# Seven block products for eight in a two-layer decoder trunk on one Trainium2 core

## The chip, the cores and the metric

The kernel runs on one core of one Trainium2 chip. The metric is device time in microseconds, from one launch to its end. In the profile PE is the matrix engine, PEld its weight loads (they overlap PE), DVE the vector engine, ACT the scalar engine, POOL the general engine, and SP the engine whose queue issues this kernel's DMAs.

## The reference: what is computed

A trunk of two residual layers over 2048 tokens of width 1024, float32, then a final normalisation. The second layer, which the change rewrites, uses dilated window attention in three groups of (window, dilation) and six heads of 128; each group has q, k and v of its own. Both layers also attend to 256 memory tokens with four heads of 64, multiply everything by a SiLU gate and project back. Cut to that layer:

```python
DIL_GROUPS = ((128, 1), (512, 4), (2048, 16))
def dilated_mixer(h, w_in):
    for g, (window, dil) in enumerate(DIL_GROUPS):
        base = g * 3 * 768
        qkv = (h @ w_in[:, base:base + 2304]).reshape(B, T, 3, 6, 128)
        q = partial_rope(qkv[:, :, 0], pos)      # rotates the first 32 of 128 rows of a head
        k = partial_rope(qkv[:, :, 1], pos)
        o, lse = dilated_group(q, k, qkv[:, :, 2], window, dil)
        ...
    wts = softmax(stack(lses), axis=0)           # over the three groups
    o = einsum('gbth,gbthd->bthd', wts, outs)
    q_mem, gate = split(h @ w_in[:, 6912:], [256])
# for each layer:
    branch = concat([mix, mem_o]) * silu(gate)
    x = x + branch @ w_out[i]
```

The second layer's input projections are a product of 2048 x 1024 by 1024 x 8192: 6912 columns for q, k and v, 256 for the memory queries, 1024 for the gates.

## The kernel before

Precision is kept by splitting each float32 operand into a high and a low fp16 half. `mm3` (L174 to L177) then makes one product of three matmuls: high by high, high by low, low by high.

**First layer** (to 913.7 us). Gated linear attention in blocks of 128 tokens, then a second pass over the 16 blocks: memory queries and memory attention (`a2_q`), gates (`a2_gate`), the branch transposed on PE (`a2_branch`), the output projection (`a2_out`). `a2_h2` normalises the block, transposes it on PE (`split_T`, L162) and writes it, split, into `h2T`, which stays in SBUF for the whole second layer.

**Second layer, units** (913.7 to about 2264 us). A unit is a pair of heads and a group, nine in all, in the order of three head pairs by three groups. For each:

- `load_qk` and `load_v` fetch three weight blocks of 1024 x 256 through the one buffer `stg` and split them (`load_w`: squares for a scale, then high and low).
- `proj_qk` projects q and k for one head: weights stationary, 512 tokens moving, 24 matmuls for each of four token chunks. The first 32 rows are rotated chunk by chunk (DVE L808, POOL L809, DVE L810 and L811), and the halves go to SBUF in the group's order (ACT L813, DVE L814).
- `proj_v` projects v for both heads: tokens stationary (every 1st, 4th or 16th, by the group), 256 weight columns moving, 24 matmuls for each of 16 blocks, evicted by ACT L786 and DVE L787.
- `attend` does one head in blocks of 128 queries against one or two blocks of keys: scores, masked maximum (DVE L843), exponential (ACT L854), split into halves (ACT L168, POOL L169), a DMA transpose through SP (L170), and the product with v. Results go to DRAM (`o_d`, L875).

Program order in a unit is attention of the first head, projection of the second head's q and k, attention of the second head, projections of the next unit. The framework's planner orders each engine's instructions by priority in program order and by a timeline of its own, so projections fill the waits of attention.

**Gates.** `gate_prep` works out the three groups' weights for a head pair. `gate_item` makes one head and chunk of 512 tokens: 24 matmuls, SiLU, then the three groups' results are read back (`og`) with their weights (`fb`), multiplied (POOL L940 and L945, DVE L942), summed (DVE L948, L949), multiplied by the gate (DVE L951) and stored. There are 24 such items. Eight are placed in unit (1, 0), eight in the last unit and eight in the stage after it, where the 16 blocks of memory attention and eight gate items of the memory heads stand too (2264 to 2520 us).

**Output** (2520 us to the end). 16 blocks of 128 tokens by 1024 columns in a rounded float32 type, three matmuls a product, then the residual and the final normalisation. Half of its weights are fetched in the stage before.

All DMAs go through SP's queue, in order.

Of the kernel before, what the change touches and what calls it, by code (L numbers as in the profile page):

```python
# [16 lines left out]
P = 128  # L17
# [17 lines left out]
def trunk(ctx, tc, a, out):  # L35
# [38 lines left out]
    cols = tl(cp, [P, 160], F32, "cols")  # L74
# [99 lines left out]
    def mm3(o, sh, sl, mh, ml, first, last):  # L174
        PE.matmul(o, sh, mh, start=first, stop=False)  # L175
        PE.matmul(o, sh, ml, start=False, stop=False)  # L176
        PE.matmul(o, sl, mh, start=False, stop=last)  # L177
# [58 lines left out]
    def mem_scores(mem, q2, wk, tg, hls):  # L236
# [3 lines left out]
        for j in range(4):  # L240
            PE.transpose(t[:, j * P:(j + 1) * P], q2[:, j].rearrange("p a d -> p (a d)"), id16)
# [4 lines left out]
        for hh in range(2):  # L246
# [9 lines left out]
            p_ = tl(wk, [P, 512], F32, tg[1 + hh])  # L256
# [58 lines left out]
    f_d = [tl(dram, [4, 3, 512], F32, f"fd{h}") for h in range(6)]  # L315
    kv_d = tl(dram, [2, 4, P, 512], F16, "kvd")
    br_d = [tl(dram, [P, 4, KT, P], F32, f"brd{c}") for c in range(4)]


    pa_ctx = ctx.enter_context(ExitStack())  # L320
    wp = pa_ctx.enter_context(pool("wpa", 5))
# [281 lines left out]
    h2T = tl(h2p, [P, 2, KT, T], F16, "h2T")  # L603

    with ExitStack() as c2:
        wo_p = c2.enter_context(pool("wo", 1, "right"))
# [11 lines left out]
        def a2_q(b):  # L618
# [6 lines left out]
            mem_pv(mem0, mem_scores(mem0, qm, k2, ("qmT", "mp", "mpt"), ((stg, "stg"), (sga, "stg"))), om, ps_g)  # L625
# [35 lines left out]
        def a2_out(b, bT, it):  # L661
            cj = tl(sp, [P, 4], F32, "cj")
            V.tensor_scalar(out=cj, in0=iwo, scalar1=it, scalar2=None, op0=ALU.mult)
            xt = tl(k1, [P, D], F32, "x")
# [12 lines left out]
        def a2_h2(b, xt):  # L677
            r = rstd_of(rowss(xt, k2), 1, D)
            xn = tl(k1, [P, D], F32, "sg")
            V.scalar_tensor_tensor(out=xn, in0=xt, scalar=r, in1=nw1, op0=ALU.mult, op1=ALU.mult)  # L680

            def emit(k0, k1_, t):
                tv = t.rearrange("p (k n) -> p k n", n=P)
                hi = h2T[:, 0, k0:k1_, b * P:(b + 1) * P]
                A.activation(out=hi, in_=tv, func=AF.Copy)
                V.tensor_tensor(out=h2T[:, 1, k0:k1_, b * P:(b + 1) * P], in0=tv, in1=hi, op=ALU.subtract)
            split_T(xn, KT, emit)
# [10 lines left out]
        xt = None  # L698
        for b in range(NB):
            bT = a2_branch(b, om, gt[0], gt[1])  # L700
            it = gt[2]
            if b + 1 < NB:
                hT, om = a2_q(b + 1)
                gt = a2_gate(hT)
            xo = a2_out(b, bT, it)
            if b > 0:
                a2_h2(b - 1, xt)
            xt = xo
        a2_h2(NB - 1, xt)
    pa_ctx.close()  # L710

# [457 lines left out]
```

## Time and profile before

| what | value |
|---|---|
| median of 2 runs | 2721.89 us (2721.33 to 2722.46) |
| profiled execution: time | 2715.5 us |
| its span, first to last instruction | 2713.5 us |
| granted TensorE clock, mean | 0.989 |
| PE busy | 2603.2 us (96%), 19166 matmuls |
| DVE, ACT, POOL busy | 1510.0, 1128.4, 496.9 us |
| DMA | 259.23 MB, mean 96 GB/s |

A row of a stretch gives its start and end, its length, then for each engine the busy time and, as x, the instructions; then the granted clock, the mean busy share of the 16 DMA engines and GB/s. A row of a group gives line, engine, operation, output <- inputs, shapes and count; after the bar the busy time in us and the mean ns of one; after the second bar the engine's idle time just before them and what ended it. Matmuls are pipelined, so the mean duration of one is longer than the distance to the next. A row of a timeline gives start and duration in us, the idle time before it in brackets. A row of one line gives the least, median and largest duration in ns and the first and last start. A row of waits gives the total, the times and the longest.

### The profile page before, as it was taken

The page shows a single profiled execution, that of the slowest core. Times are in us where ns is not written, and L with a number is a line of the kernel's source. Part 1 is how long each engine was busy: PE and PEld are TensorE (multiplying, and loading weights), DVE is VectorE, ACT ScalarE, POOL GpSimd, SP SyncE. Part 2 cuts the span into 40 slices and gives each one's busy share as a digit, 9 for nine tenths or more (in the row PEclk, how much of TensorE's full clock was granted, in tenths as well). Part 3 has the DMA queues.
Part 4 walks back from the last instruction along what each step waited for, and adds up shares of the span by engine and source line. Part 5 has one row for each costly group of instructions (what it writes and reads, how often), then busy time and mean ns, then how long its engine had stood idle before and what let it go on. Part 6 is the DMA issues. An engine that isn't in the chain of part 4 may idle for free. (4 is left out here: it accounts for less than half of the span.)

```text
span 2713.5 us, 47912 instructions
## 1 busy us (share of the span) xinstructions
PE 2603.2 (96%) x19166; PEld 1937.0 (71%) x19166; DVE 1510.0 (56%) x3349; ACT 1128.4 (42%) x2621; POOL 496.9 (18%) x421
## 2 busy tenths in 40 slices
PE   7999999999999999999999998999999999788999
PEld 6889998899988845858475474756667574455687
DVE  6445443665555466373746637465555637777433
ACT  6356444543434434252425324243433434535322
POOL 0000000010101023131313314222222313443000
PEclk9999999999999999999999999999999999899999
DMA  5242113333332213130313535122322224776543
GB/s 202 84 143 74 65 57 94 119 90 96 91 96 81 91 47 86 34 90 26 87 53 100 121 86 135 38 68 73 78 62 62 72 65 128 197 172 139 158 148 114
DMA packets 377539, 259.23 MB, mean 96 GB/s; under 512 B 250674, under 2 KB 340452, under 8 KB 377316
## 3 DMA queue, kind: packets, MB, share of 16 engines
q1 hardware_dynamic: 377316, 256.17, 33.7%
q8 instruction: 150, 2.46, 0.4%
q14 instruction: 73, 0.60, 0.1%
HBM read 149.63 MB, written 60.21 MB: 77 GB/s over the span
## 5 line engine op out<-in xcount | busy, mean ns | idle before, releaser
L175 PE MATMUL ps_mm<-w,hT 128*128 128x256 f16 (+1 forms) x1408 | 387.2, 275 | 3.7 <-DVE ws L128 1.8
L176 PE MATMUL ps_mm<-w,hT 128*128 128x256 f16 (+1 forms) x1408 | 385.9, 275 | 0.0
L177 PE MATMUL ps_mm<-w,hT 128*128 128x256 f16 (+1 forms) x1408 | 385.2, 275 | 0.4 <-DVE hT L370 0.4
L175 PE MATMUL ps_mm<-h2T,w 128*128 128x512 f16 x944 | 359.2, 380 | 0.5 <-DVE qm L232 0.4
L177 PE MATMUL ps_mm<-h2T,w 128*128 128x512 f16 x944 | 358.8, 380 | 0.6 <-DVE cols L306 0.6
L176 PE MATMUL ps_mm<-h2T,w 128*128 128x512 f16 x944 | 358.9, 380 | 0.0
L809 POOL TENSOR_TENSOR sh<-sh,rope 32x512 f32<-32x512 f32 x144 | 183.2, 1272 | 629.8 <-DVE sh L808 623.3
L177 PEld LDWEIGHTS <-w 128*128 128x128 f16 x1408 | 139.1, 99 | 148.1 <-issue 3.0
L175 PEld LDWEIGHTS <-w 128*128 128x128 f16 x1408 | 138.5, 98 | 144.5 <-issue 2.4
L176 PEld LDWEIGHTS <-w 128*128 128x128 f16 x1408 | 138.5, 98 | 144.0 <-issue 2.8
L175 PE MATMUL ps_mm<-w,h2T 128*128 128x256 f16 x840 | 229.2, 273 | 0.5 <-DVE sg L301 0.5
L176 PE MATMUL ps_mm<-w,h2T 128*128 128x256 f16 x840 | 229.5, 273 | 0.0
L177 PE MATMUL ps_mm<-w,h2T 128*128 128x256 f16 x840 | 229.4, 273 | 0.0
L854 ACT ACTIVATE pm<-pm,st,cols 128x256 f32<-128x256 f32 (+1 forms) x288 | 156.2, 543 | 135.7 <-DVE st L848 134.6
L169 POOL TENSOR_TENSOR ph<-pm,ph 128x512 f16<-128x512 f32 (+2 forms) x144 | 143.5, 1001 | 291.5 <-issue 158.8
L175 PE MATMUL ps_x<-h2T,w 128*128 128x512 f16 x464 | 177.4, 382 | 0.3 <-DVE v L787 0.3
L176 PE MATMUL ps_x<-h2T,w 128*128 128x512 f16 x464 | 177.2, 382 | 0.0
L177 PE MATMUL ps_x<-h2T,w 128*128 128x512 f16 x464 | 177.1, 382 | 0.0
L169 POOL TENSOR_TENSOR stg<-mp,stg 128x512 f16<-128x512 f32 x16 | 18.5, 1159 | 833.9 <-DMA ogd<-og 457.7
L176 PEld LDWEIGHTS <-h2T 128*128 128x128 f16 x1280 | 149.4, 117 | 10.1 <-issue 2.5
L175 PEld LDWEIGHTS <-h2T 128*128 128x128 f16 x1280 | 149.5, 117 | 7.7
L176 PEld LDWEIGHTS <-hT 128*128 128x128 f16 x1408 | 138.8, 99 | 22.3 <-issue 4.1
(317 smaller groups left out, 6102.4 us busy)
## 6 DMA issues: line engine op xcount, KB each, us to landing
stg<-in_w_in_b SPq DMA_DIRECT2D x64, 512.0 KB
od<-osb SPq DMA_DIRECT2D x72, 256.0 KB
og<-od SPq DMA_DIRECT2D x72, 256.0 KB
fb<-fd SPq DMA_DIRECT2D x24, 768.0 KB
x<-in_x SPq DMA_DIRECT2D x32, 512.0 KB
hTd<-hT SPq DMA_DIRECT2D x16, 512.0 KB
hT<-hTd SPq DMA_DIRECT2D x16, 512.0 KB
x1d<-x SPq DMA_DIRECT2D x16, 512.0 KB
```

The source lines that it names most:

```text
L169: G.tensor_tensor(out=lo, in0=src, in1=hi, op=ALU.subtract)
L175: PE.matmul(o, sh, mh, start=first, stop=False)
L176: PE.matmul(o, sh, ml, start=False, stop=False)
L177: PE.matmul(o, sl, mh, start=False, stop=last)
L809: G.tensor_tensor(out=sw, in0=sw, in1=rs, op=ALU.mult)
L854: A.activation(out=p_, in_=p_, func=AF.Exp, scale=sc, bias=st[:, j:j + 1], accum_out=st[:, 16 + j:17 + j])
```

## The change

The second layer's projections become one level of a seven-product block scheme. Tokens are cut into chunk pairs, the contraction of 1024 into two halves, and 256 weight columns into two halves of 128. A half of the tokens (`hf`) takes chunks `hf` and `hf + 2`.

- `a2_pair` replaces `a2_h2`. It takes blocks m and m + 8 together, so the blocks run in the order 0, 8, 1, 9 and so on; POOL forms the sums, ACT and DVE split seven operands in `stg` and `sga`, and DMA transposes put them in place. Some go by way of DRAM (`h2_d`).
- `load_ws` replaces `load_w256` in the second layer: a weight block becomes seven split operands of 512 x 128, in a pool of nine tiles. POOL forms the sums. q and k of one head make one block, so `load_qk` is called per head.
- `sw_half` does the seven products of a half, each of 48 matmuls of 128 columns (values, memory queries) or 12 of 512 (q, k, gates), in three PSUM banks, with snapshots and sums between them. `mm_bank` turns over four banks, among them `ps_tr`, which the transposes had alone.
- `proj_qk` collects the 32 rows to be rotated from four results into one tile of 128 partitions and rotates them together. q, k and v are written to DRAM (`qk_d`, `vu_d`) and read back by `att_load` in pieces of four blocks. In the third group a piece holds every fourth token, and `blk` reads it with a step of 4.
- The value projection's moving operand has 128 columns, and its stationary rows have steps of 1 or 4.
- All gate items, the memory queries and memory attention stand in a last stage after the units, in the order written out below; `fb` and `og` are a third of their size, with two buffers each. The output weights are fetched in the output stage, and its blocks run in another order.

```diff
+        def a2_pair(m, x1, x2):
+            ha = tl(stg, [P, 4, 2, 512], F16, "stg")
+            hb = tl(sga, [P, 3, 2, 512], F16, "stg")
+            ...
+            def put(o, src):
+                hl = ha[:, o] if o < 4 else hb[:, o - 4]
+                A.activation(out=hl[:, 0, :], in_=src, func=AF.Copy)
+                V.tensor_tensor(out=hl[:, 1, :], in0=src, in1=hl[:, 0, :], op=ALU.subtract)
+                fl = hl.rearrange("p a n -> p (a n)")
+                ...
+                    SY.dma_start_transpose(h2s[0][o].rearrange("p a k t -> p (a k) t")[:, :, ts], fl)
+                else:
+                    t = tl(k1, [P, 8, P], F16, "tq")
+                    SY.dma_start_transpose(t, fl)
+                    ...
+    OPS = (0, 4, 1, 5, 3, 2, 6)
+    def load_ws(srcs, invh, joint=True, cps=None):
+        raw = tl(stg, [P, KT, 256], F32, "stg")
+        ...
+        def put(n_, src):
+            ...
+            A.activation(out=t[:, 0], in_=src, func=AF.Copy, scale=s1)
+            V.scalar_tensor_tensor(out=t[:, 1], in0=src, scalar=s1, in1=t[:, 0], op0=ALU.mult, op1=ALU.subtract)
+        put(0, b11)
+        G.tensor_tensor(out=b11, in0=b12, in1=b11, op=ALU.subtract)
+        put(4, b11)
+        ...
+    def sw_half(ops, hf, wst, g, fin):
+        def pr(t, n, first):
+            w, h = ops[n], h2s[hf][OPS[n]]
+            if wst:
+                for k in range(4):
+                    mm3(t, w[:, 0, k, :], w[:, 1, k, :], h[:, 0, k, :], h[:, 1, k, :], first and k == 0,
+                        k == 3, True)
+                return
+            for m in range(4):
+                for k in range(4):
+                    mm3(t[:, m * P:(m + 1) * P], hcols(h[:, 0, k, :], g, m), hcols(h[:, 1, k, :], g, m),
+                        w[:, 0, k, :], w[:, 1, k, :], first and m == 0 and k == 0, m == 3 and k == 3, True)
+        ...
+        ta = mm_bank()
+        pr(ta, 0, True)
+        p1 = snap(ta, "p1")
+        tb = mm_bank()
+        pr(tb, 1, True)
+        u2 = snap(tb, "u2")
+        G.tensor_tensor(out=u2, in0=u2, in1=p1, op=ALU.add)
+        pr(ta, 2, False)
+        fin(ta, 0, 0, True)
+        pr(tb, 3, False)
+        u3 = snap(tb, "u3")
+        G.tensor_tensor(out=u3, in0=u3, in1=p1, op=ALU.add)
+        tc_ = mm_bank()
+        pr(tc_, 4, True)
+        x22 = addto(tc_, u3)
+        fin(x22, 1, 1, False)
+        pr(tb, 5, False)
+        x21 = addto(tb, p1)
+        fin(x21, 1, 0, False)
+        pr(tc_, 6, False)
+        x12 = addto(tc_, u2)
+        fin(x12, 0, 1, False)
+    def store_cols(d, g, c, hl, rows, r0):
+        if g == 0:
+            SY.dma_start(d[c][rows].rearrange("p a j x -> p a (j x)"), hl[r0])
+        else:
+            for e in range(2):
+                SY.dma_start(d[:, rows, e, c, :].rearrange("j p x -> p j x"),
+                             hl[r0, e, :].rearrange("p (j x) -> p j x", j=4))
+    def gate_item(hp, sg, c, i):
+        acc = None
+        for g in (2, 1, 0):
+            fb = tl(gb, [P, 16, 32], F32, "fb")
+            ...
+            og = tl(gb, [P, 512], F32, "og")
+            ...
+            if acc is not None:
+                V.tensor_tensor(out=fb, in0=fb, in1=acc, op=ALU.add)
+            acc = fb
         sv = sg.rearrange("p (l q) -> p q l", q=16)
         V.tensor_tensor(out=sv, in0=acc, in1=sv, op=ALU.mult)
     for n, u in enumerate(units):
+        w1_ = load_qk(u, 1)
+        attend(u, 0, wqk)
+        proj_qk(u, 1, w1_)
+        ...                      # weights of the next unit
+        attend(u, 1, w1_)
+        if not last:
+            proj_qk(units[n + 1], 0, wqk)
+            proj_v(units[n + 1], wv)
+    qm_half(0)
+    qm_half(1)
+    gate_prep(0)
+    gw = load_gate(7168)
+    mem_chunk(0)
+    gate_half(gw, 0, lambda sg, c, i: gate_item(0, sg, c, i))
+    mem_chunk(2)
+    gate_half(gw, 1, lambda sg, c, i: gate_item(0, sg, c, i))
+    ...                          # the second head pair in the same way
+    gate_half(wg, 0, mem_item)
+    gate_half(wg, 1, mem_item)
+    gw = load_gate(7680)
+    gate_half(gw, 1, lambda sg, c, i: gate_item(2, sg, c, i))
+    gate_half(gw, 0, lambda sg, c, i: gate_item(2, sg, c, i))
+        porder = [4, 5, 6, 7, 12, 13, 14, 15, 0, 1, 2, 3, 8, 9, 10, 11]
```

More of the change, by code (lines that the diff above doesn't have):

```diff
@@ L768, in load_v @@
         fsc[u] = f
[L769 to L789 removed]
+        return ops
@@ L967, in mem_out, with load_gate @@
[L967 to L972 removed]
+    negs = {}
+    def load_gate(c0, invh=None):
+        w_ = load_ws([(0, w_in_b[:, c0:c0 + 256])], invh1)
+        negs[id(w_)] = neg_of(w_[1])
+        keep.append(w_)
+        return w_
@@ L1062, in trunk @@
     ch.close()
+    c3.close()
     with ExitStack() as c5:
```

556 lines of the change are left out of this document (316 added, 240 removed).

## The prediction

> **What bounds the kernel now.** I read the busy shares first, then four stretches of the span, then single rows in the stretches that the change rewrites.
>
> ```profile
> span 2713.5 us, 47912 instructions
> PE 2603.2 (96%) x19166; PEld 1937.0 (71%) x19166; DVE 1510.0 (56%) x3349; ACT 1128.4 (42%) x2621; POOL 496.9 (18%) x421
> ...
> core 0: us, PE busy (x) PEld busy (x) DVE busy (x) ACT busy (x) POOL busy (x), PEclk, DMA share, GB/s
> 480.00:913.70 433.70, 428.09 (x4056) 384.88 (x4054) 258.43 (x579) 204.82 (x438) 34.80 (x30) 0.99 0.33 95
> 913.70:2264.20 1350.50, 1323.98 (x9093) 865.09 (x9092) 761.15 (x1803) 502.18 (x1152) 356.63 (x300) 1.00 0.29 74
> 2264.20:2520.00 255.80, 215.83 (x1507) 131.12 (x1506) 185.04 (x343) 124.98 (x306) 96.49 (x67) 0.95 0.67 162
> 2520.00:2713.50 193.50, 181.70 (x815) 147.91 (x813) 71.96 (x91) 53.89 (x127) 2.77 (x2) 0.97 0.40 139
> ```
>
> The stretches are the first layer's second half, the nine units of the second layer, its end with memory attention, and the output projection. PE is busy for 428 of 434, 1324 of 1350 and 182 of 193 us, so in three of the four every matmul saved is time saved. The third is different: PE 84%, DVE 72%, and 40 us in which PE has nothing. The execution took 2715.5 us, 2.0 more than its span and 6.4 less than the median of the runs, 2721.89.
>
> **The change, part by part.** First the matmuls, whose pace I take from distances between starts, because the durations in the rows overlap.
>
> ```profile
> 1089.83 0.38 PE L177 MATMUL ps_mm<-h2T,w 128*128 128x512 f16 x1
> ...
> 1094.37 0.38 PE L177 MATMUL ps_mm<-h2T,w 128*128 128x512 f16 x1
> ```
> ```profile
> 1245.00:1275.00 30.00, 30.00 (x277) 1.00 0.00 1
> ```
> ```profile
> 1357.37 0.22 PE L175 MATMUL ps_g<-k,q 128*128 128x128 f16 x1
> ...
> 1358.32 0.22 PE L177 MATMUL ps_g<-k,q 128*128 128x128 f16 x1
> ```
>
> The first two rows are the ends of 22 back-to-back matmuls of 512 columns: 4.54 / 21 = 0.216 us each. The stretch at 1245 lies inside a value projection and has only 256-column matmuls: 30 / 277 = 0.108. The last two rows are the ends of 18 matmuls of 128 columns, each with its own weight load: 0.95 / 17 = 0.056. So the pace is proportional to the columns, down to 128.
>
> Before, q, k and gates take 9 x 2 x 2 x 4 x 24 + 8 x 4 x 24 = 4224 matmuls of 512 columns, values and memory queries 10 x 16 x 24 = 3840 of 256: 912 + 415 = 1327 us. After, seven products stand for eight. The first group has 3696 of 512. The second must use blocks 128 columns wide, so 20 halves x 7 products x 48 = 6720 of 128: 798 + 376 = 1174 us. **153 us of PE work go.** All of it was on the path, in the units above all.
>
> The 0.056 is the doubtful price, since no run of more than 18 such matmuls stands in the trace. For two groups of units the stationary rows are also taken with a step of 4.
>
> ```profile
> L175 PEld LDWEIGHTS <-h2T 128*128 128x128 f16 x92 | 13.2, 144 | 0.0
> ```
> ```profile
> L175 PEld LDWEIGHTS <-h2T 128*128 128x128 f16 x92 | 10.4, 113 | 0.0
> ```
> ```profile
> L175 PEld LDWEIGHTS <-h2T 128*128 128x128 f16 x77 | 7.5, 98 | 0.9
> ```
>
> These are weight loads of value projections with steps 16, 4 and 1: 144, 113 and 98 ns. With step 1 loads follow each other every 56 ns in the run of 18, although each is 98 ns long, so at most 56 of it is occupancy; step 4 adds 15. The price lies between 0.056 and 0.108 (half the columns cannot cost more than all); I take 0.056, whose rows have exactly this shape. The Trainium skill, "TensorE: Matmul & The Clock Gate", section "Back-to-back issue gap", gives about 81 ns for a sustained stream of load and matmul at 128 columns; by it the 6720 would take 544 us, more than the 415 of before. The 18 matmuls here do not agree with it, but they are a short run.
>
> Layer one: the 128 transposes of the h2 blocks on PE go to the DMA.
>
> ```profile
> 911.23 1.04 PE L162 MATMUL ps_tr<-ident,sg 128*128 128x128 f32 x8
> ```
>
> Eight take 0.9 to 1.0 us, so 16 blocks save 15 us. `a2_pair` now fills `stg` and `sga`, which memory attention's high and low halves need too, and seven DMA transposes must leave first. Their issue is dear:
>
> ```profile
> L170 SPq DMA_TRANSPOSE pt<-ph x144: 1188/1232/3202, 999.2 to 2330.1; - x144
> ...
> L875 SPq DMA_DIRECT2D od<-osb x72: 320/348/2239, 1013.0 to 2340.8; - x72
> ...
> L938 SPq DMA_DIRECT2D og<-od x24: 529/550/1597, 1193.4 to 2469.6; - x24
> ```
>
> Seven at 1.23 are 8.6 us of SP, with splitting and landing some 15; PE has the next block's gate and output matmuls (2 x 96 x 0.108 = 21 us) over it. I charge 1 us a pair, 8 in all (0 to 30). At the end nothing covers: the first weights wait for `stg`, load, are squared, scaled and split, about 15 us more than now (5 to 30). The units then start at 913.7 - 15 + 8 + 15 = 922.
>
> Units: q and k 3024 x 0.216 = 653, values 6048 x 0.056 = 339, attention unchanged at 2700 times 128 columns x 0.056 = 151 (from the block counts 31, 28 and 16 a head): 1143 us of PE. What hides the rest? Each half now evicts through three snapshots, three sums and five splits, not four evictions and four rotations.
>
> ```profile
> L786 ACT ACTIVATE v<-ps_mm 128x512 f16<-128x512 f32 x46 | 27.4, 597 | 187.5 <-PE ps_mm L177 187.5
> ...
> L787 DVE SCALAR_TENSOR_TENSOR v<-ps_mm,v 128x512 f16<-128x512 f32 x47 | 32.4, 690 | 143.2 <-ACT v L786 143.0
> ```
>
> At 0.6 on ACT and 0.69 on DVE a q/k half costs 9 x 0.6 = 5.4 and 11.5 x 0.69 = 7.9, a value half 4.2 and 4.8; seven-operand weight preparation is about 7.5 and 5.5 a load. Over 36 + 18 halves, 28 loads and attention's own 285 and 225 that is some 780 us of ACT and 740 of DVE beside 1143 of PE: covered, though ACT's share rises from 37% to two thirds. The new tie is the bank: product 3 of a half waits for the snapshot of product 1, 5 for that of 3, each with one product (2.6 us) over it.
>
> SP is the tighter queue. In a unit with dilation 16 it issues some 190 plain DMAs (64 stores for values, 64 for q and k, 16 for rotated rows and tables, 24 loads for attention, the rest as before), at 0.35 to 0.55 us each by the rows above, and 16 transposes: about 95 us of issuing against 121 of PE; dilation 4 has 150 of them and 87 us, dilation 1 116 and 63. It is one queue in order, and behind a store that waits for its split stand the transposes of attention. So I take PE 5% idle in the units (2% now, 3 for banks and SP; 2 to 12 possible): 1143 / 0.95 = 1203. The units end at 2125.
>
> Last stage: now all 24 head gates stand here; 16 of them lay under units before.
>
> ```profile
> 2371.74 1.96 POOL L940 TENSOR_TENSOR fb<-og,fb 128x512 f32<-128x512 f32 x1 [2.43 <-DMA fb<-fd]
> ...
> 2483.60 2.06 POOL L940 TENSOR_TENSOR fb<-og,fb 128x512 f32<-128x512 f32 x1 [1.03 <-DMA fb<-fd]
> ```
> ```profile
> 2442.70 0.62 SPq L934 DMA_DIRECT2D fb<-fd  x1
> ...
> 2447.79 1.99 POOL L940 TENSOR_TENSOR fb<-og,fb 128x512 f32<-128x512 f32 x1 [9.13 <-DMA fb<-fd]
> ```
> ```profile
> POOL fb L940 <- DMA fb<-fd: 202.4, 22, 36.4
> ```
> ```profile
> L945 POOL TENSOR_TENSOR fb<-og,fb 128x512 f32<-128x512 f32 x13 | 22.7, 1745 | 15.8 <-DVE e L293 8.0 <-DMA fb<-fd 7.8
> ...
> L948 DVE TENSOR_TENSOR fb<-fb 128x512 f32<-128x512 f32 x13 | 15.8, 1217 | 5.0 <-POOL fb L945 4.9
> L951 DVE TENSOR_TENSOR sg<-fb,sg 128x512 f32<-128x512 f32 x14 | 15.5, 1105 | 0.1
> L942 DVE TENSOR_TENSOR fb<-og,fb 128x512 f32<-128x512 f32 x13 | 15.1, 1165 | 19.6 <-DMA fb<-fd 19.6
> ```
>
> The first pair are the first and last of eight items: 111.86 / 7 = 16.0 us an item, not because of DVE or PE but because one buffer goes through load (5.1 us from issue to use for 768 KB), two products on POOL, sums, and load again. After, `fb` and `og` have two buffers of a third the size, and the chain of one item is: load about 3, POOL 2.0, POOL 1.7, sum 1.2, next load into the freed buffer 3, product 1.1, sum 1: 13 us. PE needs 18.1 / 4 = 4.5 of it, DVE 6. Below it could be 10, if SP gives the loads early; above, today's 16. So: memory queries 672 x 0.056 = 38 us, under which the last head's attention ends; 15 for `gate_prep`, whose tiles take the place of attention's; 24 x 13 = 312, with memory attention beside it; 8 memory items at PE's 4.7 = 38; less 45, since the last half's sums wait in SBUF and the output stage begins with the half that is done: 358, to 2483. Then about 15 until output weights, formerly loaded early, are split (0 to 30), and 193.5 as now: 2692.
>
> The sum is 2692 + 2.0 = 2694 against 2715.5: **21 us less**, 2701 against the median.
>
> **Rivals.** (1) *The last stage flows.* If the two buffers give 11 us an item (48 less) and PE idles 3% in the units (25 less), it is 2628; at 10 us and 2%, 2590. For it: DVE and PE both have room. Against: the same chain holds today with PE and DVE waiting. (2) *SP's queue takes over*, the case on the other side. Priced at 0.62 an issue plus 0.1 between issues, and 1.3 a transpose, units cost (116, 150, 190 plain) 104, 129 and 158 us, 130 on average, over PE's 127 and 1172 in all; with a tenth lost to waits in order, 1300, which is 97 more: about 2800. It decides once a plain issue costs more than about 0.6. For it: the issue rows reach 2.2 us where the DMA engines are loaded. The Trainium skill, "DMA: Bandwidth & Descriptors", gives 512 B as the least transfer at line rate, with read-modify-write below it; 256 B stores are what dilations 4 and 16 now issue, and no row here shows such a store. (3) *Narrow matmuls run at the pace of weight loads.* At 0.081, the pace in the skill's section above, 6720 x 0.025 = 168 more: 2869. It decides from 0.056 + 21 / 6720 = 0.059. Against it: the run of 18. That the count of products isn't what the change says I hold for excluded by the code.
>
> **How the numbers follow.** Forecast 2701 (2665 to 2750) with 0.38; rival 1 with 0.36; rival 2 with 0.19; rival 3 with 0.07. About 2% is what a measurement here can tell from no change: faster 0.36, same 0.38, slower 0.26. The range leaves out rival 3, the worst of rival 2 and the best of rival 1: 2595 to 2810.
>
> **What would show it.** Right: about 21500 matmuls, value projections at 56 ns from start to start, units of 1180 to 1230 us, and a last stage of about 360 with PE near 62% and POOL waiting for `fb`. Rival 1 shows in first products closer than 12 us; rival 2 in attention waiting long for `pt`, evictions waiting for `hl`, and an SP without gaps; rival 3 in narrow matmuls over 60 ns apart. I am wrong altogether if the planner moves gate items under the units, or if the stretch before 900 changes by more than 25 us.

## The result and the profile after

The changed kernel takes 3279.43 us (median of 3270.76 and 3288.09), against 2721.89: 1.2048 times as long, 95% interval 1.1911 to 1.2186. The forecast was 2701 us, its range ended at 2810. The profiled execution took 3288.09 us, 2.1 more than its span.

First the head of the page and the stretches of the span, with the borders put where the stages now change (columns as before).

```profile
span 3286.0 us, 56046 instructions
...
PE 2580.2 (79%) x21354; PEld 1907.2 (58%) x21354; DVE 1663.1 (51%) x3375; ACT 1434.0 (44%) x3095; POOL 764.0 (23%) x601
...
480.00:906.00 426.00, 401.74 (x3707) 355.93 (x3706) 268.96 (x569) 198.82 (x430) 75.67 (x57) 0.97 0.56 131
906.00:981.00 75.00, 32.51 (x341) 28.41 (x340) 25.00 (x40) 18.14 (x34) 14.08 (x10) 0.70 0.81 234
981.00:2500.00 1519.00, 1270.13 (x11639) 846.84 (x11636) 803.47 (x1729) 749.51 (x1552) 518.37 (x403) 0.94 0.57 146
2500.00:3090.00 590.00, 239.97 (x1201) 121.58 (x1202) 262.08 (x420) 180.67 (x372) 146.76 (x107) 0.66 0.46 113
3090.00:3286.00 196.00, 185.23 (x792) 149.07 (x792) 70.61 (x89) 45.61 (x113) 2.84 (x2) 0.96 0.39 135
```

Three marks are read in every kernel below. The first, 981 here, is the start of the first matmul that reads a row operand kept in a `wo` tile. It stands inside the first half of the units: their very first product starts at 968.4. In the other kernels, too, the mark comes 12 to 14 us after the first product, except in the two with plain products, where it comes 24 to 25 us after it. The second mark is the copy of the last attention block (2500), the third the first output matmul (3090). No engine is busy for more than 53% in the units except PE, and PE's 1270 is flattered by records that overlap: counted by starts at 0.216, 0.108 and 0.056 us a matmul, its work there is 1171 us, so 348 are lost. The row shows 249 of them as idle time.

The table goes by the very first product. (The forecast counted from a border at 913.7 in the kernel before; there the first products of the units were already under way from 905.7.)

| stage | forecast | measured | over |
|---|---|---|---|
| first product of the units | 922 | 968 | 46 |
| units, to the last attention block | 1203 | 1532 | 329 |
| to the first output matmul | 358 + 15 | 590 | 217 |
| output | 193.5 | 196 | 2 |

What PE waited for, in the units and then in the last stage (total, times, longest):

```profile
PE ps_g L789 <- ACT w L781: 61.9, 3, 30.3
PE ps_o L175 <- DMA pt<-ph: 59.2, 45, 3.3
PE ps_g L175 <- DVE mx L1034: 26.5, 31, 2.6
PE ps_tr L175 <- ACT w L808: 16.1, 5, 7.7
PE ps_g L175 <- DMA k<-qkd: 14.3, 7, 5.1
```
```profile
PE ps_o L277 <- DMA mp<-mh: 180.9, 29, 12.6
PE ps_x L175 <- ACT w L1262: 86.6, 1, 86.6
```

The profile lists some 150 waits of PE in the units: most are of 5 us or less, and two are of 30. One of the two, near 1399, shows how a queue does it (rows of SP, ACT and PE from the timeline):

```profile
1330.51 1.62 SPq L768 DMA_DIRECT2D stg<-in_w_in_b  x3
...
1351.62 42.05 SPq L951 DMA_DIRECT2D vud<-hl  x61
1393.72 0.60 SPq L768 DMA_DIRECT2D stg<-in_w_in_b  x1
1394.36 0.50 SPq L994 DMA_DIRECT2D q<-qkd  x1
...
1397.46 1.06 ACT L781 ACTIVATE w<-stg 128x1024 bf16<-128x1024 f32 x1 [17.42 <-DMA stg<-in_w_in_b]
...
1398.66 0.58 PE L789 MATMUL ps_g<-rm,ones 128*128 128x2 f32 x2 [29.78 <-ACT w L781]
```

Three of the four parts of a weight load are issued at 1330. Then 61 stores of dilation-16 values in a row hold SP for 42 us, and behind them stand the fourth part and attention's own loads. ACT waits for the weights, and PE stands for 29.8 us at the matmul that sums their squares, with attention behind it in its order. The other wait, of 30.3 us near 2384, stands behind a run of 61 stores in the same way.

### The profile page after: what moved, and what is told of

Same layout as the page of the kernel before. It is cut to its first block, busy times and chain, and to the rows that moved or that the text cites. A ratio compares the mean times of both kernels' runs of the same rounds, so it can differ in the third digit from the quotient of the medians.

```text
span 3286.0 us, 56046 instructions
## 1 busy us (share of the span) xinstructions
PE 2580.2 (79%) x21354; PEld 1907.2 (58%) x21354; DVE 1663.1 (51%) x3375; ACT 1434.0 (44%) x3095; POOL 764.0 (23%) x601
## 5 line engine op out<-in xcount | busy, mean ns | idle before, releaser
L176 PEld LDWEIGHTS <-w 128*128 128x128 f16 x2032 | 211.7, 104 | 202.2 <-issue 87.3
L175 PEld LDWEIGHTS <-w 128*128 128x128 f16 x2032 | 212.8, 105 | 173.3 <-ACT w L808 38.8
L177 PEld LDWEIGHTS <-w 128*128 128x128 f16 x2032 | 211.5, 104 | 164.6 <-issue 21.7
L809 DVE SCALAR_TENSOR_TENSOR w<-stg,ws,w 128x512 f16<-128x512 f32 x224 | 196.5, 894 | 89.1 <-ACT w L808 88.6
L927 ACT ACTIVATE hl<-cx 128x512 f16<-128x512 f32 x162 | 137.9, 852 | 225.8 <-DVE cx L846 144.0
L928 DVE SCALAR_TENSOR_TENSOR hl<-cx,hl 128x512 f16<-128x512 f32 x162 | 160.0, 990 | 149.7 <-ACT hl L927 139.7
L808 ACT ACTIVATE w<-stg,ws 128x512 f16<-128x512 f32 x224 | 152.8, 715 | 94.3 <-POOL stg L820 25.2
L175 PE MATMUL ps_mm<-w,w 128*128 128x128 f16 (+1 forms) x740 | 185.1, 280 | 6.7 <-DVE cx L846 4.1
L176 PE MATMUL ps_mm<-w,w 128*128 128x128 f16 (+1 forms) x740 | 184.8, 280 | 0.0
L177 PE MATMUL ps_mm<-w,w 128*128 128x128 f16 (+1 forms) x740 | 184.6, 279 | 0.0
L277 PE MATMUL ps_o<-vm,mp 128*128 128x128 f16 x128 | 22.0, 273 | 180.9 <-DMA mp<-mh 180.9
L855 POOL TENSOR_TENSOR u<-u,p 128x512 f32<-128x512 f32 x64 | 91.2, 1426 | 281.9 <-ACT u L841 266.0
L176 PEld LDWEIGHTS <-hT 128*128 128x128 f16 x1408 | 139.2, 99 | 25.1 <-issue 6.5
L175 PEld LDWEIGHTS <-hT 128*128 128x128 f16 x1408 | 139.7, 99 | 21.0 <-issue 2.1
L177 PEld LDWEIGHTS <-hT 128*128 128x128 f16 x1408 | 139.6, 99 | 18.3 <-DVE hT L374 0.7
L277 PEld LDWEIGHTS <-mp 128*128 128x128 f16 x192 | 22.5, 122 | 205.6 <-issue 173.3
```

The source lines that it names most:

```text
L175: PE.matmul(o, sh, mh, start=first, stop=False, skip_group_check=free)
L176: PE.matmul(o, sh, ml, start=False, stop=False, skip_group_check=free)
L177: PE.matmul(o, sl, mh, start=False, stop=last, skip_group_check=free)
L277: PE.matmul(ov2[:, :, j * 64:(j + 1) * 64], pth[:, ts], vm[:, :, vs], start=m == 0, stop=False)
L808: A.activation(out=t[:, 0], in_=src, func=AF.Copy, scale=s1)
L809: V.scalar_tensor_tensor(out=t[:, 1], in0=src, scalar=s1, in1=t[:, 0], op0=ALU.mult, op1=ALU.subtract)
```

## The experiments

**Theories.** Q: SP's one queue in order is too full, and loads and transposes stand behind stores. S: the seven products' snapshots, sums and banks hold PE up. W: the preparation of seven weight operands does. C: the matmul of the squares does, because it stands ahead of attention in PE's order. M: memory attention holds the last stage up. "Units" is from the first mark to the last attention block (1519; the first four expectations begin a little ahead of the first product and say 1537), "last stage" from there to the first output matmul (590). The expectations call the first mark the first product. Each kernel of this section was run once, the last one four times. Kernels whose code for a stage is that of the changed kernel gave 1503 to 1520 for its units, 578 to 599 for its last stage, and 953 to 968 for the very first product, so differences of 15 to 20 us mean nothing here.

**1. Eight plain products.** `sw_half` runs four blocks of two products, with no snapshot and no sum; `load_ws` splits four quarters.

```diff
-        ta = mm_bank(); pr(ta, 0, True); p1 = snap(ta, "p1") ...
+        for ci in range(2):
+            for ni in range(2):
+                t = mm_bank()
+                pr(t, ni, 2 * ci, True)
+                pr(t, 2 + ni, 2 * ci + 1, False)
+                fin(t, ci, ni, True)
```


> Changed kernel with eight plain products of half-size blocks in the place of the seven (no snapshots, no sums of products, no sums of weights; the products' operands are the stored blocks of the rows as they are, so the values are not those of the reference). PE work in the units rises by a seventh of the products: q and k 3456 x 0.216 = 746, values 6912 x 0.056 = 387, attention 151: 1284 us. Theory A (the way of q, k, v through DRAM, with its stores and loads on SP's one queue, holds PE up): the waits stay, units about 1284 + 300 = 1590, a little more than the 1537 of the changed kernel. Theory B (the seven products' banks, snapshots and sums hold PE up): the waits go, units about 1330, although there is more PE work. Theory C (the matmul that sums the weights' squares waits in PE's order): as A, 1590.


Units 1452 (2436 - 984), with waits of 162 us instead of 348. Neither A nor B alone. Because the mark stands elsewhere in this kernel, the comparison is made from the very first product: 1477 against 1532, so 55 less, with 131 more PE work (1313 against 1182) and 186 less waiting. The seven products save 131 us of PE and cost 186.

**2. Without the stores.** `store_cols` and the value stores return at once; `att_load` reads `h2_d`.


> Changed kernel without the stores of q, k and v to DRAM (evictions and splits stay); attention loads tiles of the same size from a tensor that was written long before, so its values are not those of the reference. Theory A: units fall from 1537 to about 1240 (1195 of PE work and 4% idle). Theory B: the evictions still hold the banks, units stay within 40 of 1537. Theory C: as B. If the queue is only one part, the units land between, and the part is what is missing.


Units 1425 (2399 - 974): 94 less. Q is a part. The two waits of 30 us are gone. (The loads of this kernel also read a tensor that lies otherwise in DRAM, so a share of the gain could be theirs.)

**3. No sum of squares on PE.** `tot = rm[:, 0:n]` in the place of the matmuls.


> Changed kernel without the matmul that sums the squares of a weight block over partitions; each partition takes its own sum (not the reference's scale), so ACT goes on without PE and PE never waits for ACT's squares. Everything else stays. Theory C: the 71 us of waits ahead of this matmul go and with them what stood behind, units 1537 down to 1400 to 1470. Theories A and B: the wait moves to the first product that reads these weights or to the attention next to it, units within 25 of 1537.


Units 1436 (2410 - 974): 83 less, as C says. But attention's waits for `pt`, `mx` and `k`, 100 us together in the changed kernel, are 143 here. The two waits of 30 at the squares are gone, but one of 29 stands at attention's keys instead:

```profile
PE ps_g L175 <- DMA k<-qkd: 35.3, 6, 29.0
```

**4. No memory attention.** `mem_chunk` returns; `mem_item` loads rows of `x1_d`.


> Changed kernel without memory attention in the last stage (scores, softmax, values, turning; the memory gates multiply a tensor written earlier, so the values are not the reference's). The stage from the last attention block to the first output matmul takes 585 us now. Theory M (PE stands in order behind memory attention's transposes, 181 us of waits, and the gate products come late): stage 420 to 460, that is 24 items at 15.5 plus 8 memory items, the queries and the gap ahead of the output. Theory G (the gate items' chain through loads and POOL sets the pace by itself): within 40 of 585.


Last stage 407 (2881 - 2474): 183 less, about as much as the 180.9 of PE's waits. M holds. The gate items then mostly follow each other every 14 to 18 us.

**5. Weight loads issued by ACT.** In `load_ws`: `SY.dma_start(raw...)` becomes `A.dma_start(raw...)`.


> Changed kernel, its results kept, with the loads of the second layer's weight blocks (4 DMAs a block) issued by ACT and not by SP. From the first product of the units to the last attention block the changed kernel takes 1519 us (981 to 2500). Theory Q (the weight loads stand in SP's queue behind the runs of stores; PE then waits at the matmul that sums the squares): the two waits of 30 us and most of the 71 us ahead of these matmuls go, units 1430 to 1455. Theory D (the load or the squares wait for a free buffer, the staging tile or one of the nine operand tiles): units within 20 of 1519.


Units 1460 (2437 - 977): 59 less, 5 above the range of Q and far from D. The two waits of 30 us are gone, and that is the whole gain.

**6. Seven products, no sums of them.** `fin` after each of four fresh banks (2, 2, 2 and 1 product).


> Changed kernel with its seven products and seven weight operands, but without the snapshots and sums of products: the products run in four fresh banks (2, 2, 2 and 1 product), and each bank is split straight from PSUM as in the plain form (values not the reference's). PE work stays at 1171 us. Theory S (snapshots, sums and the handing over of banks hold PE up): the waits fall to those of the plain form, about 160, and the units take 1330 to 1365. Theory W (the preparation of seven weight operands, with sums on POOL and nine tiles, holds PE up): units 1470 to 1519. In between, the parts are as the time divides.


Units 1423 (2400 - 976): 96 less. In between: without sums and handed-over banks 96 go, and the 265 of waits that stay (1159 of PE work stand in this stretch) are some 100 more than with plain products, which have four weight operands instead of seven.

**7. Memory attention threaded between gate products.** Behind each finished gate block: values and turn of one query block, scores of the next.


> Changed kernel, its results kept, with memory attention of the last stage threaded between the gate products: behind each finished block of gates the values of one query block are taken and the scores of the next computed, so that a gate product lies between the issue of a transpose and its use. Nothing is left out. The stage from the last attention block to the first output matmul takes 589 us now and 407 without memory attention. Theory M (the 181 us are PE standing in order behind the transposes): 410 to 450. Rival (memory attention's work on DVE, ACT and SP delays the gate items by itself): 500 to 560.


Last stage 571 (3066 - 2495). A miss: PE still waited 173 us for `mp`. A half's seven products are 18 us of PE and four query blocks' waits are far longer, so there was little to put between; M's remedy as I had thought of it does next to nothing.

**8. Thirteen operand tiles,** no memory attention: `pool("wq", 13)`.


> The kernel without memory attention in the last stage (which makes the room), with thirteen operand tiles for weights instead of nine. Beside the run without memory attention, whose units take 1503 us. Theory D (a block's squares and operands wait for the tiles of the block before): the 71 us ahead of the sums of squares go, units 1420 to 1450. Theory Q (the loads stand in SP's queue): within 20 of 1503.


Units 1497 (2462 - 966) beside 1503: no D. And yet the waits at the squares nearly went (now in the row of PE's waits at L787), and others grew by nearly as much, the transposes' for one. Two rows of PE's waits in this kernel's units:

```profile
PE ps_o L175 <- DMA pt<-ph: 65.2, 51, 3.0
...
PE ps_g L787 <- ACT w L781: 8.5, 9, 4.0
```

A wait that names one cause can be a place where several late chains meet. A run of 61 stores stands here as before (1345 to 1388), but the four parts of the weight load now stand together behind it (1400).

**9. Three groups of DMAs on ACT's queue:** the transposes in `a2_pair`, memory attention's transposes and stores, the output stage's row loads.


> Changed kernel, its results kept, with three groups of DMAs issued by ACT and not by SP: the transposes of the row blocks' seven sums in the first layer, the transposes and stores of memory attention in the last stage, and the loads of branch and residual rows in the output stage. Each is read in its own stage. Theory Q (SP's one queue in order): memory attention's transposes no longer stand behind gate loads that wait for a buffer, their waits of about 12.6 us fall to some 4 and the stage from the last attention block to the first output matmul goes from 589 to 440 to 490; the 87 us without a matmul ahead of the output stage shrink to 20 to 40. Rival (buffers: the transposes wait for their own tiles, the output's loads for tiles of the stage before): stage within 30 of 589, gap 70 to 90. Start: with Q the first product of the units comes at 955 to 965, with buffers (memory attention's halves share two tiles with the sums) at 975 to 985.


All three against Q: first mark 1014, later by 33, which is outside both ranges; last stage 594 (3122 - 2528); gap ahead of the output 84.7. In the last stage memory attention waits as before:

```profile
PE ps_o L278 <- DMA mp<-mh: 195.5, 29, 13.6
```

What it waits for is read from one block of the changed kernel, rows of PE, ACT, POOL and SP between two turns:

```profile
2579.24 0.66 PE L1167 MATMUL ps_tr<-ident,om 128*128 128x128 f32 x2 [1.48 <-DVE om L286]
...
2580.85 0.40 PE L251 MATMUL ps_g<-kk,qmT 128*128 128x256 f16 x1 [0.52 <-DVE qmT L242]
...
2582.32 0.42 PE L252 MATMUL ps_g<-kl,qmT 128*128 128x256 f16 x1
...
2582.97 0.56 ACT L259 ACTIVATE mp<-ps_g,mmx,cols 128x256 f32<-128x256 f32 x1 [2.65 <-DVE mmx L255]
...
2585.86 1.15 POOL L169 TENSOR_TENSOR mh<-mp,mh 128x512 f16<-128x512 f32 x1 [11.81 <-ACT mh L168]
...
2587.04 5.92 SPq L170 DMA_TRANSPOSE mp<-mh  x2
...
2589.84 0.63 ACT L168 ACTIVATE mh<-mp 128x512 f16<-128x512 f32 x1 [4.06 <-DMA mp<-mh]
2589.90 0.27 PE L277 MATMUL ps_o<-vm,mp 128*128 128x128 f16 x1 [7.16 <-DMA mp<-mh]
...
2594.59 0.26 PE L277 MATMUL ps_o<-vm,mp 128*128 128x128 f16 x1 [3.90 <-DMA mp<-mh]
...
2596.87 0.45 PE L1167 MATMUL ps_tr<-ident,om 128*128 128x128 f32 x1 [1.48 <-DVE om L286]
```

From turn to turn 17.63 us, and in all of it one thing after another: turn, scores, maxima, exponentials, halves, transpose, values. The second half starts at 2589.84 only when the first has left the one tile `mh`, and the next block's scores follow the values in PE's order. POOL had been idle for 11.8 us and ACT for 4: no engine is short. Sixteen blocks of it are 282 us.

**10. Plain products and no stores** together.


> Eight plain products in the place of the seven, and no stores of q, k and v (attention loads other tensors; values not the reference's). Alone the plain form takes 1452 us in the units (1290 of it PE work) and the form without stores 1425 (1158 of it PE work), against 1519. If the two causes add up: 1290 + 162 - 94 = 1358, the level of the kernel before, 1350. If they share their waits: 1400 to 1440.


Units 1422 (2407 - 985): 30 less than plain alone (31 from the very first product). The causes share their waits; they do not add up.

**11. No stores, and weight loads on ACT.**


> The seven products in full, without the stores of q, k and v (values not the reference's), and with the weight loads issued by ACT. Alone the first saves 94 us in the units, the second 59. If the weight loads were late because of the stores ahead of them in SP's queue, the second adds little here: 1405 to 1425. If both count by themselves: 1366. What is left over the PE work of 1171 is what the sums and the attention's own chain cost without the queue.


Units 1384 (2363 - 979): 135 less, where 153 would be both in full.

**12. Stores on POOL, weight loads on ACT.**


> Changed kernel, its results kept: all stores of q, k and v issued by POOL, all weight loads by ACT, so SP keeps only loads and transposes. Theory Q: the units come near the form without stores, 1400 to 1440. Rival (POOL's time for some 1100 issues delays its sums of products and weights, or the transfers themselves cost): 1480 or more.


Units 1513 (2492 - 979). The rival: POOL is busy for 931 us there, 412 more, in 745 more instructions, which are the stores (128, 80 and 40 a unit by dilation, 744 in all) at some 0.55 us each. That the transfers themselves cost it, the other half of the rival, is answered by run 17. Here, too, PE's waits for the squares fell, from 68 us to 16, and others grew by as much.

```profile
979.00:2492.00 1513.00, 1291.38 (x11625) 859.39 (x11622) 859.57 (x1730) 748.51 (x1555) 930.71 (x1148) 0.94 0.55 146
```

**13. No weight sums on POOL.** The seven operands are taken from the quarters.


> Changed kernel without the four sums of weight quarters on POOL; the seven operands are written from the quarters as they are (values not the reference's), so ACT and DVE write them without waiting for POOL. Units of the changed kernel: 1519 us. Theory W (ACT and DVE stand in order behind POOL's sums in each of 28 preparations, some 4 to 6 us each, and attention and evictions stand behind them): 1400 to 1450. Otherwise (the waits come from the queue and from the sums of products): 1490 to 1519.


Units 1427 (2399 - 972): 92 less, in the range of W. ACT's waits show two places. Its waits for POOL's sums, 46 us in the changed kernel, are gone, and its wait for the load is 56 us shorter. First four rows of the changed kernel, then one of this one:

```profile
ACT w L781 <- DMA stg<-in_w_in_b: 124.4, 36, 17.4
...
ACT w L808 <- POOL stg L820: 17.5, 9, 4.0
ACT w L808 <- POOL stg L815: 14.8, 14, 2.0
ACT w L808 <- POOL stg L812: 14.1, 14, 2.2
```
```profile
ACT w L781 <- DMA stg<-in_w_in_b: 68.7, 31, 7.2
```

But PE's waits for the squares went from 68 us to 7, and this is two thirds of the 92. The run of stores that had caused them is as long as before. What changed is the place of the load in SP's order, whole and behind the stores:

```profile
1329.78 44.56 SPq L942 DMA_DIRECT2D vud<-hl  x64
...
1386.50 2.13 SPq L768 DMA_DIRECT2D stg<-in_w_in_b  x4
```

PE does not stand at the squares there. In runs 2, 5, 6, 16 and 17, too, the waits for the squares are 2 to 14 us instead of 68, so 54 to 67 of each gain are the same waits, the two of 30 above all. In the changed kernel they came from one order that the planner chose, three parts of a load ahead of the stores and one behind. What else goes is about 39 (run 2), 28 (run 6), 31 (run 13) and 26 (run 17), not far above the noise, and nothing in runs 5 and 16.

**14 and 15. Weight work between attention's blocks,** its load issued as soon as the staging tile is free; in the second kernel by ACT.

```diff
-        w1_ = load_qk(u, 1)
-        attend(u, 0, wqk)
+        attend(u, 0, wqk, {2: m1})        # m1: load_qk(u, 1) on a tile loaded before
```


> Changed kernel, its results kept, with the work on a weight block (squares, scale, sums, operands) moved from ahead of attention to between two of its four blocks, and the load of the next block's weights issued as soon as the staging tile is free, so ahead of the stores of the next projection. Theory O (order: on PE the sum of squares, on ACT and DVE the operands stand ahead of attention's own steps and wait for a late load): the 71 us ahead of the sums go and part of attention's 124, units 1400 to 1450. Theory Q alone (stores ahead of attention's loads and transposes): 1450 to 1480, since only the weight load gets out of their way, as with the loads on ACT (1460).

> As the kernel with the weight work moved between attention blocks, its results kept, with the weight loads issued by ACT. If the early issue has already taken the loads out of the stores' way: within 15 us of that kernel's units. If SP's queue as such still holds them: 25 to 50 less.


Units 1678 (2653 - 975) in both: 159 more. The first is a miss for both theories; the second, within 15 of the first, agrees with the early issue having taken the loads out of the stores' way. PE now waits for the keys themselves:

```profile
PE ps_g L175 <- DMA k<-qkd: 187.2, 14, 26.9
```

In the changed kernel that row is 14.3. By the program order, the weight work had stood between the second head's projection and its attention, and now nothing does. I read this as the way of k through DRAM, up to 27 us from projection to attention, which the weight work had covered. No run takes the detour away by itself, so this reading is argued and not shown.

**16. Two blocks of memory attention in flight.** Scores of the next block before the values of this one; `mh` and a second tile `mi`; four `mp`; seven operand tiles, for room. (The edit to the first layer that the expectation names is not in this kernel; it is in the last one.)

```diff
+            if pend:
+                done()                     # mem_pv, mem_turn of the block before
+            pend.append((p_, sn))
```


> Changed kernel, its results kept, with two edits in separate stages. Last stage: the scores of the next query block of memory attention are computed before the values of the present one, with two tiles for the halves and four for the transposed ones (seven operand tiles for weights instead of nine make the room, so the units are not compared). A block now takes 17.7 us from scores to scores. If that is one serial chain: two in flight give 9 to 11 us a block, and the stage goes from 589 to 460 to 490. If it is an engine's or queue's time: 550 or more. First layer: memory attention's halves get tiles of their own and no longer share two with the seven sums. If that sharing delays the first layer, its last sum comes at 906 to 912 instead of 931 and the first product of the units at 950 to 962 instead of 981; if it is the work of the transposes and their stores, 925 to 931 and 972 to 981.


Last stage 483 (2920 - 2436): 107 less, in the range of the serial chain. PE waits for the two tiles 49 us instead of 181:

```profile
PE ps_x L175 <- ACT w L1270: 113.3, 1, 113.3
PE ps_o L277 <- DMA mp<-mh: 34.8, 12, 8.3
...
PE ps_o L277 <- DMA mp<-mi: 14.6, 8, 4.7
```

Unlooked for, the units take 1462 with seven operand tiles, 57 less than with nine. Fewer tiles change the planner's order. The waits taken away are the two of 30 us: PE waits 8 us for the squares here instead of 68.

**17. The dilation-16 values in another order in DRAM,** so that a split block goes out in 2 stores instead of 8.

```diff
-                for r in range(4):
-                    for e in range(2):
-                        SY.dma_start(vd[ni][:, c * 32:(c + 1) * 32, e, r, :] ..., hl ... [r][:, e, :] ...)
+                for e in range(2):
+                    SY.dma_start(rows.rearrange("j (p e) x -> e p j x", e=2)[e], hl[:, e, :] ...)
```


> Changed kernel, its results kept, with another order of the dilation-16 values in DRAM, so that 16 stores a unit take the place of 64 and 16 loads of values that of 8; the bytes and the 256-byte packets stay. If SP's time for issues is the cost (a run of some 50 stores took 34 us): 3 x 40 x 0.65 = 78 us of it go and the units, 1519 now, take 1430 to 1480; the two waits of 30 us at a sum of squares go. If the way through DRAM (landing, packets) is the cost: 1500 to 1525.


Units 1434 (2412 - 978): 85 less, with the same bytes (438.6 MB in both kernels) in 16,500 more packets, since the loads of these values now come in smaller pieces. The stores' rows, least, median and most ns of an issue, of the changed kernel and of this one:

```profile
L951 SPq DMA_DIRECT2D vud<-hl x192: 576/602/1851, 1341.3 to 2379.2; - x192
```
```profile
L951 SPq DMA_DIRECT2D vud<-hl x48: 359/442/1899, 1335.7 to 2300.1; - x48
```

192 x 0.60 less 48 x 0.44 is 94 us of SP's time, and 24 more loads at 0.58 take 14 back: the units gained about what SP no longer spends on issuing. The bytes are the same and the packets more, so this group's transfers were not its cost. But 58 of the gain are the two waits behind the runs of stores. So the agreement of the sums is partly luck: as I read it, what counted is that a load no longer stood behind 42 us of issues, not every issue saved.

**18. Together:** run 16, run 17's order, memory attention's halves in the first layer in tiles of their own, and the output's row loads by ACT into `wp`'s tiles.


> The kernel with two blocks of memory attention in flight and seven operand tiles (3109 us), its results kept, with three edits more. First layer: memory attention's halves in tiles of their own; if the sharing delays it, its last sum comes at 906 to 912 instead of 923 to 931 and the first product of the units at 950 to 962 instead of 975; if not, no change. Units: the other order of the dilation-16 values; 1462 without it, 1390 to 1430 if issues are the cost. Output: the loads of branch and residual rows by ACT into tiles that hold row sums of the second token half, free before the last gate products; if the 113 us without a matmul ahead of the output stage are a wait for buffers, 25 to 40 are left and the stage from the last attention block to the first output matmul goes from 483 to 395 to 415; if not, 470 or more. In all 2930 to 2990 if all three hold, so still slower than the kernel before, since 24 gate items of 15 us and PE's waits in the units stay.


2988.29 us, 1.1024 times the time of before (1.1006 to 1.1043), at the upper end of what was expected. Units 1402 (2374 - 972), last stage 423 (2796 - 2374, 395 to 415 expected), the gap 56 instead of 113 (25 to 40 expected). With run 9, where another queue alone left 85: it was a wait for tiles, in good part. The first layer's last sum comes at 920. It came at 914 to 931 in the kernels without this edit, run 9 apart, so there is no gain from tiles of its own. In the first layer PE waits no less for the transposes than before, now from the unshared tiles; the first row is of the changed kernel, the second of this one:

```profile
PE ps_g L277 <- DMA mp<-stg: 12.5, 7, 2.9
```
```profile
PE ps_g L277 <- DMA mp<-m: 19.3, 7, 4.4
```

By elimination, the sums' transposes and stores themselves are what is late there. No run shows it by itself, and why ACT's queue made it worse (run 9) stays open.

## Why the prediction was wrong

**PE's work was right.** 21354 matmuls against some 21500, and the narrow ones at 0.056: in a value projection of the changed kernel 96 weight loads and matmuls start in 5.30 us (three matmuls more were still under way).

```profile
1363.40:1368.70 5.30, 5.30 (x99) 5.30 (x96) 1.44 (x3) 0.09 (x1) 0.00 (x0) 1.00 0.19 41
```

5.30 / 96 is 0.055. Rival 3 is refuted, in runs of 48. By count and price the 153 us did go.

**"Covered" is the step that failed in the units.** I set 780 us of ACT and 740 of DVE beside PE's 1143, found room and charged 3% for banks and SP. The engines' sums were about right (750 and 803 measured), but a sum of busy time says nothing of order. PE lost 348 us, not 60. By what goes with each part alone: sums of products and banks 96, weight sums on POOL 92, stores 94, weight loads behind stores 59. They are not to be added, and they are not four separate causes: 54 to 67 of each are the same waits, the two of 30 us above all (run 13), and runs 10 and 11 show more that is shared. What is shown as a whole is run 1: without sums of products and with four operands a block, PE waits 164 us instead of 350 (counted from the very first product). How the rest of the 350 divides between bank, queue and operands stays open. Both ties that I named, the bank and the queue, are there; the one that I did not name is the weight block: staging tile, load, squares, PE's sum, seven operands in a row, ahead of attention on three engines.

**Rival 2 had the sign and a part of the mechanism.** It put 97 us on SP's queue, and without the stores 94 go, with the weight loads off the queue too 135. That the two sums are so close is luck. The rival decides once a plain issue costs more than about 0.6 us. Of the stores only those of the dilation-16 values do, with a median of 0.602; the 1387 plain issues of the units have a mean of 0.51, inside the 0.35 to 0.55 that I had taken. With 144 transposes at 1.40, SP issues for 914 us of the 1532, so its queue as a whole is not full. That the stores would stand in one run of sixty ahead of a part of a load I had not placed. The Trainium skill, "Trainium Kernel Development and Optimization", section "Key Constraints", says that issuing DMAs from several engines saves only the sequencer's issue time. The runs here agree as far as they go: the weight loads on ACT, 94 in the units, won 59 us (run 5), and 744 stores on POOL won nothing, since their time moved to an engine that had no room (run 12).

**Last stage.** 24 items at 13 were forecast, 15 measured: 48 us at most. The step that failed is "with memory attention beside it": one serial chain of 17.6 us a block in PE's order, worth 183 of the 217. The output stage was to overlap the last items and save 45 us; instead PE stands for 87 us ahead of it, in good part because its tiles lie where those of the last items lie (run 18).

**Start.** 1 us a pair and 15 for the first weights were both too little. The last sum came 25 us later than before (931 against 906) instead of 7 earlier: if the 15 us of saved transposes are right, the pairs cost 40 us instead of 8, beyond the 30 that I allowed. Other kernels with the same first layer had it 8 to 23 later. The first product came 37 us after the last sum instead of some 23, of which PE waited 34 for the first weights' squares; that is inside the range given. The stated sign "wrong altogether if the stretch before 900 changes by more than 25 us" came true by a hair in this execution and not in the others. Output: 193.5 forecast, 196 measured.

Rival 1 fell with the items' 15 us and with the 23% of the units that PE loses.

## What to carry to other kernels

Before calling work covered, write its chain down in order, engine by engine, and ask what stands behind each wait in PE's and the queue's order; busy sums bound the time only from below. Count a queue's issues by run, not by average: the same bytes in a quarter of the DMAs were worth 85 us, while moving DMAs to another engine's queue won 59 alone and 41 on top of run 2, and otherwise did nothing or harm. Before crediting an edit with a gain, look which wait went: six different edits here removed the same two waits, some by what they were made for and some only because the planner ordered the queue otherwise. A block algorithm that saves an eighth of the matmuls may pay more for its sums in waits than it saves where the products are only 2.6 us long: here plain products, on all else of the changed kernel, were 55 us faster in the units.

## What was not expected of the hardware

PE ran at half its clock where it had waited. In the memory block above, seven steps of 256-column matmuls take from 2580.85 to 2582.32, 0.21 us each, where the kernel before had 0.108; the granted clock is 0.50 there, 0.66 in the last stage and 0.94 in the units. At the start of the units, after a wait of 34.3 us and three short ones, 128-column matmuls start 0.107 us apart from 969.23 to 972.64, and 0.056 apart after it. The Trainium skill, "TensorE: Matmul & The Clock Gate", section "HAM oscillation — how this bites in real kernels", tells of the same: short bursts between waits start at half rate each time. In the units, starts that came late by less than 0.15 us, to which slow matmuls belong, add up to some 35 us against some 11 before, so this was a small part of the loss. An issue's price depended on the form of the store: 0.60 us for 4 x 32 pieces of 256 bytes, 0.44 for 4 x 128 pieces, four times the bytes.
